# Hybrid encoder step: attention products of 64 rows made with 128 rows

## The chip, the cores and the metric

The kernel runs on one core of one Trainium2 chip. A core has a matrix engine, TensorE (PE in the profile, its weight loads PEld), two engines that work on rows of 128 partitions, VectorE (DVE) and ScalarE (ACT), a programmable engine, GpSimd (POOL), and SyncE (SP), which issues DMAs. Each engine takes its instructions in order; semaphores hold an instruction until another engine's is done. TensorE multiplies a stationary operand of up to 128 rows and 128 columns (the weights, loaded by an instruction of their own) with a moving one; the rows are the partitions over which the product is summed. The metric is the device time of the program in microseconds (us), lower is better.

## The reference

One step of a two-layer streaming encoder: 512 tokens of a new stream (the prompt) and 64 tokens of a running one (the sample, with 256 cached keys). Layer 0 joins a matrix memory and retention, layer 1 is latent attention with 8 heads, and a SwiGLU network and a layer norm follow each. The change is in layer 1's attention:

```python
def block(args):
    qn, qr, qp = args
    s = jnp.einsum('bqhd,bkhd->bhqk', qn, k_nope) + jnp.einsum('bqhr,bkr->bhqk', qr, kr_all)
    s = s.astype(jnp.float32) * MLA_SCALE
    vis = k_chunk[None, :] <= (qp // CHUNK)[:, None]
    p = jax.nn.softmax(jnp.where(vis, s, -jnp.inf), axis=-1).astype(v.dtype)
    return jnp.einsum('bhqk,bkhv->bqhv', p, v)
```

A head's query and key have a part of 128 (`qn`, `k_nope`) and a rotary part of 64 (`qr`, `kr_all`, the key's part being the same for all heads). `CHUNK` is 64: a block of 128 queries sees all keys up to its end, except that its first 64 queries don't see the last 64 keys.

## The kernel before

All products are made in pieces: an operand is split into a high part (fp32r) and a low part (what is left of it), and a product is the sum of high x high, high x low and low x high. The 576 tokens stand in five tiles: tile 0 is the sample with 64 tokens, tiles 1 to 4 are the prompt with 128 each. Weights come from memory by DMA, ScalarE and VectorE (or GpSimd, in the stretch of the attention, `lo_engine`) split them into the two parts (line 364 and 362), and a ring of slots holds them.

In the attention each head has three kinds of work. `heads(h)` makes its keys and queries (`kn_units`, `qn_units`) and brings the rotary queries into place (`qr_unit`): `qrt[h % 2]` has 128 partitions, in one half the high part of the 64 rotary values, in the other half their low part; for odd heads the halves are swapped (`p0 = 64 * (h % 2)`). The rotary keys stand twice, in partitions 0 to 63 and again in 64 to 127: `kk` has the high part, `self.kl[0]` the low part. `values(p)` makes the values of two heads: `vt[0]` and `vt[1]` have the two parts for seven tiles of keys (`KTILE`); the third of them holds the sample's last keys, 64 rows of them.

`attn(h)` spawns one task per tile, and each has three steps:
- `sa(i)`: the scores. Five products go into one bank: three of 128 rows for the large part, one of 128 rows with `kk` (queries' high and low part with the keys' high part), and one of 64 rows, the queries' high part with the keys' low part (line 1958). For the prompt's tiles a sixth product of one row (line 1960) adds -1e30 to the last 64 keys of the first 64 queries: `mrow` is a row of bf16 numbers, made at the kernel's start. Then VectorE takes the maximum (line 1963), ScalarE the exponential (1964), and GpSimd or VectorE divides by the sum (1967).
- `sb(i)`: TensorE transposes the probabilities (line 533), ScalarE and VectorE split them into two parts (1879, 1880). For the sample these are `pt0`, with three blocks of keys; of the third only 64 rows are written.
- `sc(i)`: probabilities times values. For the sample there are nine products, of which the three with the last keys have `w` = 64 rows.

The order of all this is written once, when the program is made: the tasks yield to a planner that adds up an assumed time of each product (`clk` in `mm`) and resumes a task when its lag is over. The recorded order then stands in each engine's queue.

Of the kernel before, what the change touches and what calls it, by code (L numbers as in the profile page):

```python
# [8 lines left out]
F32 = mybir.dt.float32  # L9
F32R = mybir.dt.float32r  # L10
BF16 = mybir.dt.bfloat16
# [17 lines left out]
NEG = -1.0e30  # L29
# [188 lines left out]
class Kern:  # L218
# [335 lines left out]
    def setup(self):  # L554
        nc, t = self.nc, self.t
        self.lead = LEAD
        self.lo_engine = nc.vector
        self.tk = TK0
        self.Z = self.st("Z", [128, KT * NTOK])
        self.T0 = self.st("T0", [128, T0_N])  # L560
        self.T1 = self.st("T1", [128, T1_N])
        self.Xh = self.st("Xh", [128, KT * NTOK], F32R)
        self.Xl = self.st("Xl", [128, KT * NTOK], F32R)
        self.H = self.st("H", [128, 2 * KT * NTOK], F32R)
        self.small = self.st("small", [128, 480])
        self.sm_at = 0
        self.ident = self.st("ident", [128, 128])
        self.ones = self.st("ones", [128, 128])
        self.cvec = self.st("cvec", [128, 4])
        self.lnv = self.st("lnv", [128, 4, 2, 8])  # L570
        self.gv = self.st("gv", [128, 8])
        self.mask = self.st("mask", [128, 2, 128])
        self.rope = self.st("rope", [128, 2, NT, 64])
        self.cst = self.st("cst", [128, 12])
        self.bif = self.st("bif", [128, 8])
        self.mrow = self.st("mrow", [1, 192], BF16)
        nc.gpsimd.memset(self.ones, 1.0 / 1024.0)
        nc.gpsimd.memset(self.cvec[:, 0:2], 1.0 / 1024.0)
        nc.gpsimd.memset(self.cvec[:, 2:4], 1.0 / 512.0)
        nc.gpsimd.memset(self.mrow[:, 0:64], 1.0)  # L580
        nc.gpsimd.memset(self.mrow[:, 64:128], 0.0)
        nc.gpsimd.memset(self.mrow[:, 128:192], NEG)
        wg = self.T0[:, 4300:4364]
        self.wgp = self.st("wgp", [128, KT, 16], F32R)
        for j in range(4):
            for k in (2 * j, 2 * j + 1) if j == 0 else (2 * j,):
                e = k + 1 if j == 0 else k + 2
                nc.sync.dma_start(half_view(self.Z, 0, k, e), half_dram(t["x"], 0, k, e))
                if j < RAW and k % 2 == 0:
                    self.dma_w(j, 2 if j == 0 else 1)  # L590
        nc.gpsimd.dma_start(wg, t["wg"])
        for name in ("rope", "mask", "cst", "ident"):
            nc.gpsimd.dma_start(getattr(self, name), t[name])
        nc.gpsimd.dma_start(self.bif, t["b_if"].to_broadcast([128, 8]))
# [1068 lines left out]
    def layer1(self):  # L1663
        nc, t = self.nc, self.t
        V, A, G = nc.vector, nc.scalar, nc.gpsimd
        T0, H = self.T0, self.H
# [195 lines left out]
        pt0 = knt[1][:, :, 832:1024].rearrange("p b (j q) -> p b j q", j=3)  # L1862
        qnt = [T1r[:, 832 + 1152 * j:832 + 1152 * (j + 1)].rearrange("p (a t) -> p a t", a=2) for j in range(2)]
        qrt = [T1r[:, 3136 + 576 * j:3712 + 576 * j] for j in range(2)]
        KTILE = [(0, 128), (128, 128), (256, 64)] + [(320 + 128 * j, 128) for j in range(4)]

        late = []
# [70 lines left out]
        def attn(h):  # L1938
            qn, kn = qnt[h % 2], knt[h % 2]
            qs = qrt[h % 2]  # L1940
            p0 = 64 * (h % 2)
            vc = 128 * (h % 2)
            obank = {}

# [3 lines left out]
            def sa(i):  # L1948
                L, s = TLEN[i], TSTART[i]
                k0, k1, _ = keys(i)  # L1950
                n = k1 - k0
                x = self.xbank()
                ps = x[0:L, 0:n]
                self.mm(ps, qn[:, 0, s:s + L], kn[:, 0, k0:k1], True, False)
                self.mm(ps, qn[:, 0, s:s + L], kn[:, 1, k0:k1], False, False)
                self.mm(ps, qn[:, 1, s:s + L], kn[:, 0, k0:k1], False, False)
                self.mm(ps, qs[:, s:s + L], kk[:, k0:k1], False, False)
                self.mm(ps, qs[p0:p0 + 64, s:s + L], self.kl[0][p0:p0 + 64, k0:k1], False, i == 0)
                if i:
                    self.mm(x[:, n - 64:n], self.mrow[:, 0:128], self.mrow[:, 128:192], False, True)  # L1960
                nm, den = self.smalls(1)[0:L], self.smalls(1)[0:L]
                P = Pb[(5 * h + i) % 3][0:L, 0:n]
                V.tensor_reduce(nm, ps, AX.X, ALU.max, negate=True)
                A.activation(P, ps, AF.Exp, bias=nm, accum_out=den)
                flush()
                V.reciprocal(den, den)
                (G if i in NP else V).tensor_scalar(P, P, den, None, ALU.mult)
# [25 lines left out]
            def sc(i):  # L1993
# [15 lines left out]
                for gi, (c, n, q0, ts, j0) in enumerate(groups):  # L2009
                    seq, late = [], []  # L2010
                    for j, tt in enumerate(ts):
                        w = KTILE[tt][1]
                        vh, vl = vt[0][0:w, tt, vc:vc + 128], vt[1][0:w, tt, vc:vc + 128]
                        a, b = full[0][0:w, j0 + j, q0:q0 + n], full[1][0:w, j0 + j, q0:q0 + n]
                        seq += [(vh, a), (vl, a)]
                        late.append((vh, b))
                    seq += late
# [227 lines left out]
```

## Time and profile before

| | before |
|---|---|
| median of 3 runs | 1423.02 us (1422.81 to 1429.33) |
| the profiled execution | 1427.26 us |
| its span, first to last instruction | 1425.3 us |
| TensorE busy | 1387.2 us (97%) |
| VectorE, ScalarE, GpSimd busy | 971.2, 611.9, 171.1 us |
| attention of layer 1 | 800 to 956 us of the span |

The profile is of one execution. The ends of TensorE's products are modelled, and they overlap: the sum of their lengths says little, and what a product costs is read from the start of the one behind it. Most of TensorE's products are issued from one line (465, in the helper `mm`) and all transposes from line 533, so that they are told apart by the names of their operands and by their shape.

### The profile page before, as it was taken

The numbers are of one execution on the slowest core, as the hardware profiler recorded it, in microseconds if no ns is written. First come the engines' busy times: TensorE is split into PE (matmuls) and PEld (weight loads), VectorE is DVE, ScalarE is ACT, GpSimd is POOL, SyncE is SP. The second block draws the span as 40 slices with busy tenths as digits, with TensorE's granted clock in tenths as the row PEclk, the third lists the DMA queues.
The fourth block names the chain that finished last, engine by engine and source line by source line (L and its number), as shares of the span: only waits on it lengthen the run. The fifth ranks groups of instructions, "written<-read, shape, count | busy, mean of one in ns | idle before, by whom it ended". The sixth has DMA issues, their size and how long they took to land.

```text
span 1425.3 us, 24687 instructions
## 1 busy us (share of the span) xinstructions
PE 1387.2 (97%) x9787; PEld 1312.4 (92%) x9787; DVE 971.2 (68%) x2252; ACT 611.9 (43%) x1295; POOL 171.1 (12%) x203
## 2 busy tenths in 40 slices
PE   7999999999999999999999999999999999999995
PEld 5767999998999999999987888889899999999995
DVE  5645577767973576488898555557888458747876
ACT  4411333435551353255354455543555235415543
POOL 5200010104200000000021433310230000000000
PEclk9998999999999999999999999999999999999998
DMA  6111121522233122322321100012212313322221
GB/s 213 60 60 37 60 60 60 176 70 60 75 104 104 60 89 91 102 89 91 116 84 57 33 28 31 31 47 73 89 45 89 135 45 105 104 77 87 90 74 67
DMA packets 37314, 112.91 MB, mean 79 GB/s; under 512 B 4504, under 2 KB 11608, under 8 KB 37200
## 3 DMA queue, kind: packets, MB, share of 16 engines
q1 hardware_dynamic: 36656, 110.33, 23.2%
q8 instruction: 76, 1.25, 0.3%
q0 software_dynamic: 544, 1.02, 0.2%
q14 instruction: 38, 0.31, 0.1%
HBM read 107.45 MB, written 3.89 MB: 78 GB/s over the span
## 4 chain that ended last, share of the span: by engine, by line
PE 86%; DVE 8%; ACT 2%; DMA 1%; issue 1%; POOL 1%; SPq 0%; POOLq 0%; ACTq 0%; DVEq 0%
PE mm L465 45%; PE x L465 38%; PE x L533 2%; DVE r L362 1%; DVE Z L1270 1%; PE o L465 1%; DVE Z L1256 1%; DMA raw<-in_w 1%; ACT Xh L1302 1%; DMA Z<-in_x 0%; ACT Z L1309 0%; ACT r L364 0%; DVE small L543 0%; DVE small L542 0%; DVE small L541 0%
## 5 line engine op out<-in xcount | busy, mean ns | idle before, releaser
L465 PE MATMUL mm<-H,r 128*128 128x320 f32 (+2 forms) x2832 | 388.6, 296 | 0.0
L465 PEld LDWEIGHTS mm<-H,r 128*128 128x128 f32 x2832 | 379.1, 188 | 0.7
L465 PE MATMUL x<-Xh,r 128*128 128x288 f32 x1216 | 243.6, 295 | 0.0
L465 PE MATMUL mm<-Xh,r 128*128 128x288 f32 (+2 forms) x1152 | 232.1, 299 | 6.1 <-DVE Z L1176 2.7
L364 ACT CAST r<-raw 128x512 fp32r<-128x512 f32 (+2 forms) x292 | 178.0, 646 | 110.1 <-PE mm L465 78.9
L362 DVE TENSOR_TENSOR r<-raw,r 128x512 fp32r<-128x512 f32 (+2 forms) x276 | 195.8, 738 | 41.7 <-ACT r L364 38.0
L465 PE MATMUL x<-r,r 128*128 128x288 f32 (+3 forms) x1534 | 212.0, 293 | 0.2 <-DVE r L1046 0.2
L465 PEld LDWEIGHTS x<-r,r 128*128 128x128 f32 (+1 forms) x1534 | 205.1, 188 | 1.7 <-issue 0.7
L465 PEld LDWEIGHTS x<-Xh,r 128*128 128x128 f32 x1216 | 194.5, 188 | 0.5
L465 PEld LDWEIGHTS mm<-Xh,r 128*128 128x128 f32 x1152 | 185.4, 191 | 7.5 <-ACT Z L1309 3.4
L465 PE MATMUL x<-Xl,r 128*128 128x288 f32 x608 | 179.0, 294 | 0.0
L465 PE MATMUL mm<-Xl,r 128*128 128x288 f32 (+2 forms) x576 | 168.6, 301 | 0.0
L364 ACT CAST r<-T 128x512 fp32r<-128x512 f32 (+1 forms) x114 | 86.8, 761 | 126.9 <-DVE T L397 103.6
L465 PEld LDWEIGHTS x<-Xl,r 128*128 128x128 f32 x608 | 114.1, 188 | 0.0
L465 PEld LDWEIGHTS mm<-Xl,r 128*128 128x128 f32 x576 | 108.4, 191 | 0.1
L362 DVE TENSOR_TENSOR r<-T,r 128x512 fp32r<-128x512 f32 (+1 forms) x114 | 96.3, 866 | 17.8 <-ACT r L364 17.8
L465 PE MATMUL mm<-r,Xh 128*128 128x512 f32 (+1 forms) x320 | 100.5, 396 | 6.9 <-ACT r L364 5.8
L1310 POOL TENSOR_TENSOR Xl<-Z,Xh 128x288 fp32r<-128x288 f32 (+2 forms) x36 | 30.7, 853 | 468.0 <-ACT Z L1309 467.8
L465 PEld LDWEIGHTS mm<-r,Xh 128*128 128x128 f32 x320 | 59.8, 195 | 20.5 <-ACT r L364 6.6
L1214 ACT ACTIVATE T<-Z 128x288 f32<-128x288 f32 (+2 forms) x56 | 24.8, 443 | 92.1 <-DVE Z L1176 47.3
L465 PE MATMUL mm<-r,Xl 128*128 128x512 f32 (+1 forms) x160 | 62.2, 389 | 0.0
L1571 DVE TENSOR_TENSOR T<-T,x 128x288 f32<-128x288 f32 x38 | 17.3, 454 | 59.8 <-PE x L465 59.8
(315 smaller groups left out, 1738.8 us busy)
## 6 DMA issues: line engine op xcount, KB each, us to landing
raw<-in_w SPq DMA_DIRECT2D x169, 512.0 KB, 3.6
r<-in_w SPq DMA_DIRECT2D x20, 512.0 KB, 3.6
Z<-in_x SPq DMA_DIRECT2D x1, 1280.0 KB
o_y<-Z SPq DMA_DIRECT2D x2, 640.0 KB, 3.2
Z<-in_x SPq DMA_DIRECT2D x2, 512.0 KB, 5.9
Z<-in_x SPq DMA_DIRECT2D x1, 1024.0 KB, 8.8
o_y<-Z SPq DMA_DIRECT2D x4, 256.0 KB, 2.2
Z<-in_x SPq DMA_DIRECT2D x3, 320.0 KB, 9.3
```

Of the source, the lines that this page charges most:

```text
L362: self.lo_engine.tensor_tensor(t[:, 1], src, t[:, 0].bitcast(F32), ALU.subtract)
L364: self.nc.scalar.copy(t[:, 0], src)
L465: self.nc.tensor.matmul(out, lhsT, rhs, start=start, stop=stop, skip_group_check=more)
L533: self.nc.tensor.transpose(out, in_, self.ident[0:n, 0:n])
L1214: nc.scalar.activation(q, z, AF.Square)
L1256: V.tensor_tensor(z, z, xd[:, 0:n], ALU.subtract)
L1270: V.scalar_tensor_tensor(z, z, gain(m), R[:, 0:n], ALU.mult, ALU.mult)
L1302: A.activation(self.Xh[:, a:b], z, AF.Identity, bias=bias(m))
L1310: G.tensor_tensor(self.Xl[:, a:b], z, self.Xh[:, a:b].bitcast(F32), ALU.subtract)
L1571: V.tensor_tensor(s[:, 0:n], s[:, 0:n], ps, ALU.add)
```

## The change

The products of 64 rows and of one row in the attention are made with 128 rows.
- The low rotary product takes all 128 partitions of `qs` and of `self.kl[0]`. With it the queries' low part times the keys' low part is added, which was left out before.
- The mask is a piece of `H` with 128 partitions and 192 columns of fp32r, zero but for the first partition. The row `mrow` in bf16 and its three fills at the start are gone.
- The products of the sample's last keys take 128 rows of `vt` and of `pt0`. GpSimd fills the rows 64 to 127 of both with zeros ahead of the first head; nothing else is written there afterwards.

```diff
--- before.py
+++ after.py
@@ -573,13 +573,9 @@
         self.rope = self.st("rope", [128, 2, NT, 64])
         self.cst = self.st("cst", [128, 12])
         self.bif = self.st("bif", [128, 8])
-        self.mrow = self.st("mrow", [1, 192], BF16)
         nc.gpsimd.memset(self.ones, 1.0 / 1024.0)
         nc.gpsimd.memset(self.cvec[:, 0:2], 1.0 / 1024.0)
         nc.gpsimd.memset(self.cvec[:, 2:4], 1.0 / 512.0)
-        nc.gpsimd.memset(self.mrow[:, 0:64], 1.0)
-        nc.gpsimd.memset(self.mrow[:, 64:128], 0.0)
-        nc.gpsimd.memset(self.mrow[:, 128:192], NEG)
         wg = self.T0[:, 4300:4364]
         self.wgp = self.st("wgp", [128, KT, 16], F32R)
         for j in range(4):
@@ -1862,6 +1858,14 @@
         pt0 = knt[1][:, :, 832:1024].rearrange("p b (j q) -> p b j q", j=3)
         qnt = [T1r[:, 832 + 1152 * j:832 + 1152 * (j + 1)].rearrange("p (a t) -> p a t", a=2) for j in range(2)]
         qrt = [T1r[:, 3136 + 576 * j:3712 + 576 * j] for j in range(2)]
+
+
+        for a in [pt0[64:128, p, 2] for p in range(2)] + [t[64:128, 2] for t in vt]:
+            G.memset(a.bitcast(F32), 0.0)
+        mask = H[:, 8768:8960]
+        G.memset(mask.bitcast(F32), 0.0)
+        G.memset(mask[0:1, 0:64].bitcast(F32), 1.0)
+        G.memset(mask[0:1, 128:192].bitcast(F32), NEG)
         KTILE = [(0, 128), (128, 128), (256, 64)] + [(320 + 128 * j, 128) for j in range(4)]
 
         late = []
@@ -1938,7 +1942,6 @@
         def attn(h):
             qn, kn = qnt[h % 2], knt[h % 2]
             qs = qrt[h % 2]
-            p0 = 64 * (h % 2)
             vc = 128 * (h % 2)
             obank = {}
 
@@ -1955,9 +1958,9 @@
                 self.mm(ps, qn[:, 0, s:s + L], kn[:, 1, k0:k1], False, False)
                 self.mm(ps, qn[:, 1, s:s + L], kn[:, 0, k0:k1], False, False)
                 self.mm(ps, qs[:, s:s + L], kk[:, k0:k1], False, False)
-                self.mm(ps, qs[p0:p0 + 64, s:s + L], self.kl[0][p0:p0 + 64, k0:k1], False, i == 0)
+                self.mm(ps, qs[:, s:s + L], self.kl[0][:, k0:k1], False, i == 0)
                 if i:
-                    self.mm(x[:, n - 64:n], self.mrow[:, 0:128], self.mrow[:, 128:192], False, True)
+                    self.mm(x[:, n - 64:n], mask[:, 0:128], mask[:, 128:192], False, True)
                 nm, den = self.smalls(1)[0:L], self.smalls(1)[0:L]
                 P = Pb[(5 * h + i) % 3][0:L, 0:n]
                 V.tensor_reduce(nm, ps, AX.X, ALU.max, negate=True)
@@ -2009,9 +2012,8 @@
                 for gi, (c, n, q0, ts, j0) in enumerate(groups):
                     seq, late = [], []
                     for j, tt in enumerate(ts):
-                        w = KTILE[tt][1]
-                        vh, vl = vt[0][0:w, tt, vc:vc + 128], vt[1][0:w, tt, vc:vc + 128]
-                        a, b = full[0][0:w, j0 + j, q0:q0 + n], full[1][0:w, j0 + j, q0:q0 + n]
+                        vh, vl = vt[0][:, tt, vc:vc + 128], vt[1][:, tt, vc:vc + 128]
+                        a, b = full[0][:, j0 + j, q0:q0 + n], full[1][:, j0 + j, q0:q0 + n]
                         seq += [(vh, a), (vl, a)]
                         late.append((vh, b))
                     seq += late
```

No instruction changes its place in a queue. TensorE's queue in the first head, the end of tile 1's scores and those of tile 2, with the semaphores that are waited for (the width is that of the output, the number of rows isn't shown; `x` is the scores' bank, `T_434` and `T_433` the queries and low keys), before:

```order
L465 MATMUL x_8085<-H_74,T_434_7587 128x128
L465 MATMUL x_8085<-T_434_7587 128x128
L465 LDWEIGHTS mrow_85
L465 MATMUL x_8085<-mrow_85 128x64
L465 MATMUL x_8096<-r_454_7909,T_434_7587 128x256 [waits PE_49]
L465 MATMUL x_8096<-r_454_7909,T_434_7587 128x256 x2
L465 MATMUL x_8096<-H_74,T_434_7587 128x256
L465 MATMUL x_8096<-T_434_7587 128x256
L465 LDWEIGHTS mrow_85
```

and in the changed kernel:

```order
L465 MATMUL x_8088<-H_74,T_433_7583 128x128
L465 MATMUL x_8088<-T_433_7583 128x128
L465 MATMUL x_8088<-H_74 128x64 [waits Pool_49]
L465 MATMUL x_8099<-r_453_7905,T_433_7583 128x256 [waits PE_49]
L465 MATMUL x_8099<-r_453_7905,T_433_7583 128x256 x2
L465 MATMUL x_8099<-H_74,T_433_7583 128x256
L465 MATMUL x_8099<-T_433_7583 128x256
```

The mask is one instruction with a load like that of its neighbours, from `H`, where a bf16 load and a product stood, and its first product waits for GpSimd.

GpSimd's queue between the rotated queries (the last `T` ahead) and the low parts of the first head's weights (`r` from `raw`), before:

```order
L1851 TENSOR_TENSOR T_2_70<-T_2_70 128x512 [waits DMAHW3_49,DMAHW5_49,DVE_49,PE_49]
L1851 TENSOR_TENSOR T_2_70<-T_2_70 128x512 [waits DMAHW6_49,DMAHW4_49,DVE_49]
L1851 TENSOR_TENSOR T_2_70<-T_2_70 128x512 [waits DMAHW6_49,DMAHW7_49,DVE_49,PE_49]
L362 TENSOR_TENSOR r_27_126<-raw_442_7707,r_27_126 128x512 [waits DMAHW1_49,Activation_49]
L362 TENSOR_TENSOR r_31_175<-raw_443_7719,r_31_175 128x512 [waits DMAHW2_49,PE_49,Activation_49]
```

and in the changed kernel:

```order
L1847 TENSOR_TENSOR T_2_70<-T_2_70 128x512 [waits DMAHW6_49,DMAHW4_49,DVE_49]
L1847 TENSOR_TENSOR T_2_70<-T_2_70 128x512 [waits DMAHW6_49,DMAHW7_49,DVE_49,PE_49]
L1864 MEMSET r_454_7906 64x64 [waits Pool_49]
L1864 MEMSET r_454_7906 64x64
L1864 MEMSET r_455_7907 64x256
L1864 MEMSET r_456_7908 64x256 [waits DMASW1_49]
L1866 MEMSET H_74 128x192 [waits Pool_49]
L1867 MEMSET H_74 1x64 [waits Pool_49]
L1868 MEMSET H_74 1x64
L362 TENSOR_TENSOR r_26_122<-raw_441_7703,r_26_122 128x512 [waits DMAHW1_49,Activation_49]
L362 TENSOR_TENSOR r_30_171<-raw_442_7715,r_30_171 128x512 [waits DMAHW2_49,PE_49,Activation_49]
```

The seven fills stand ahead of three splits of weights, and none of them waits for another compute engine. The queues of VectorE, ScalarE and SyncE are the same.

## Rows read from the trace of the kernel before

**Rows 1.** The page of the profile: busy time of each engine with its share of the span, and the shares of the engines in the chain of work that ended last.

```profile
PE 1387.2 (97%) x9787; PEld 1312.4 (92%) x9787; DVE 971.2 (68%) x2252; ACT 611.9 (43%) x1295; POOL 171.1 (12%) x203
...
PE 86%; DVE 8%; ACT 2%; DMA 1%; issue 1%; POOL 1%; SPq 0%; POOLq 0%; ACTq 0%; DVEq 0%
```

**Rows 2.** The table of stretches, the one from 800 to 956 us (the attention): length, then busy time of PE, PEld, DVE, ACT and POOL with the number of instructions that started in it, then the granted TensorE clock, the DMA share and GB/s.

```profile
800.00:956.00 156.00, 156.00 (x1057) 133.89 (x1056) 83.29 (x227) 81.18 (x233) 47.28 (x45) 1.00 0.09 28
```

**Rows 3.** The timeline of TensorE (PE) in the first head, in order of time; columns: start in us, us from the first start to the last end of the row's instructions, engine, line, operation, output <- inputs, rows*columns of the weights, shape of the moving operand, count. `T` holds the scaled queries and the keys' low part (buffer T1), `r` the keys' two parts (buffer `knt`), `H` the rotary keys' high part, `x` the scores. A row of several instructions has only the first start. 802.74 to 803.41 is the sample's group, 803.70 to 804.55 that of tile 1, 804.67 to 805.66 that of tile 2; 805.79 belongs to the key projection of the next head. 810.44 lies in the group of tile 3, 811.20 begins that of tile 4, and 812.89 comes behind it.

```profile
802.74 0.60 PE L465 MATMUL x<-r,T 128*64 128x320 f32 x3
803.18 0.30 PE L465 MATMUL x<-H,T 128*64 128x320 f32 x1
803.41 0.35 PE L465 MATMUL x<-T 64*64 64x320 f32 x1
803.70 0.55 PE L465 MATMUL x<-r,T 128*128 128x128 f32 x3
804.09 0.28 PE L465 MATMUL x<-H,T 128*128 128x128 f32 x1
804.29 0.32 PE L465 MATMUL x<-T 64*128 64x128 f32 x1
804.55 0.20 PE L465 MATMUL x<-mrow 1*128 1x64 bf16 x1
804.67 0.63 PE L465 MATMUL x<-r,T 128*128 128x256 f32 x3
805.14 0.28 PE L465 MATMUL x<-H,T 128*128 128x256 f32 x1
805.35 0.38 PE L465 MATMUL x<-T 64*128 64x256 f32 x1
805.66 0.20 PE L465 MATMUL x<-mrow 1*128 1x64 bf16 x1
805.79 3.70 PE L465 MATMUL mm<-H,r 128*128 128x256 f32 x26
...
810.44 0.34 PE L465 MATMUL x<-H,T 128*128 128x384 f32 x1
...
811.20 0.97 PE L465 MATMUL x<-r,T 128*128 128x512 f32 x3
...
812.89 0.74 PE L465 MATMUL mm<-H,r 128*128 128x256 f32 x4
```

**Rows 4.** The timeline of TensorE in narrow stretches, so that a row begins with an instruction in the midst of its run: the same columns.

```profile
803.86 0.39 PE L465 MATMUL x<-r,T 128*128 128x128 f32 x2
...
806.13 0.52 PE L465 MATMUL mm<-H,r 128*128 128x256 f32 x3
...
806.49 0.58 PE L465 MATMUL mm<-H,r 128*128 128x256 f32 x3
...
810.09 0.51 PE L465 MATMUL x<-r,T 128*128 128x384 f32 x2
...
811.77 0.40 PE L465 MATMUL x<-r,T 128*128 128x512 f32 x1
812.01 0.40 PE L465 MATMUL x<-H,T 128*128 128x512 f32 x1
...
814.50 0.39 PE L465 MATMUL o<-r,r 128*128 128x64 f32 x2
```

**Rows 5.** The timeline of TensorE's weight loads (PEld) in the groups of tile 1: the same columns.

```profile
804.03 0.19 PEld L465 LDWEIGHTS x<-H,T 128*128 128x128 f32 x1
804.29 0.18 PEld L465 LDWEIGHTS x<-T 64*128 64x128 f32 x1
804.54 0.09 PEld L465 LDWEIGHTS <-mrow 1*128 1x128 bf16 x1
804.67 0.42 PEld L465 LDWEIGHTS x<-r,T 128*128 128x128 f32 x3
```

**Rows 6.** The timeline of TensorE at the nine products of probabilities and values for the sample, of the first head (814.39) with the product behind them (first of two at 815.83, third at 816.23), and of the sixth head (910.93) with the transposes behind them: the same columns.

```profile
814.39 1.51 PE L465 MATMUL o<-r,r 128*128 128x64 f32 x9
...
815.83 0.56 PE L465 MATMUL mm<-H,r 128*128 128x320 f32 x2
...
816.23 0.46 PE L465 MATMUL mm<-H,r 128*128 128x320 f32 x2
...
910.93 1.42 PE L465 MATMUL o<-r,r 128*128 128x64 f32 x9
912.29 0.44 PE L533 MATMUL x<-ident,T 128*128 128x128 f32 x2
```

**Rows 7.** The timeline of GpSimd (POOL) between the rotated queries and the first low parts of weights (the last bracket: idle time before, and what ended it), and the view of line 975, a fill: count, then shortest, median and longest duration in ns, first and last start.

```profile
791.28 1.29 POOL L1851 TENSOR_TENSOR T<-T 128x512 f32<-128x512 f32 x1 [1.09 <-PE mm L465]
792.52 1.29 POOL L362 TENSOR_TENSOR r<-raw,r 128x512 fp32r<-128x512 f32 x1
796.01 1.30 POOL L362 TENSOR_TENSOR r<-raw,r 128x512 fp32r<-128x512 f32 x1 [2.19 <-ACT r L364]
...
L975 POOL MEMSET Z<- x1: 307/307/307, 53.0 to 53.0; 64x256 f32 x1
```

**Rows 8.** The timeline of VectorE (DVE) and of TensorE at the second head's first score product: the scaled rotary queries that VectorE writes, and the product.

```profile
815.71 0.83 DVE L1920 SCALAR_TENSOR_TENSOR T<-x,T 64x320 fp32r<-64x320 f32 x2
...
817.77 0.39 PE L465 MATMUL x<-r,T 128*64 128x320 f32 x1
```

## The prediction

> **What bounds the kernel now.** I read the page's busy times and its chain of work first, then the table of stretches, then the attention instruction by instruction. TensorE is busy for 97% of the span and holds 86% of the chain that ended last [rows 1]. The change touches only the attention, 800 to 956 us. There TensorE is busy for all 156.0 us, VectorE for 83.3, ScalarE for 81.2 and GpSimd for 47.3, and the granted clock is 1.00, the upper level of 2.4 GHz [rows 2]. So TensorE's own instructions set the end here: a product that takes a shorter time on TensorE shortens the kernel, as long as nobody else becomes late.
>
> A busy TensorE doesn't mean that every product is cheap. The lengths in the rows overlap, so a product's price is read from the distance between two starts. In an undisturbed run of products of 128 rows it is 0.115 us at 128 columns and 0.12 at 256 (803.86 to 804.09 for two, 806.13 to 806.49 for three), 0.11 at 64, 0.175 at 384, 0.24 at 512 [rows 3, 4], and 0.147 at 320 (802.74 to 803.18 for three) [rows 3]. Now the scores of the first head's tile 1: three products, the one with the keys' high part, the rotary low product of 64 rows, the mask product of 1 row. From 804.09 to 804.29 passes 0.20 us instead of 0.11, from 804.29 to 804.55 0.26 instead of 0.11, the mask takes 0.12, and the first product of the next group, 256 wide, is late as well: 805.79 to 806.13 for two products, behind tile 2's mask, is 0.34 instead of 0.24 [rows 3, 4]. The weight loads show why: in an even run a load starts ahead of its product (804.03 for the product of 804.09), but the loads of the 64-row product, of the mask and of the next 128-row product start at 804.29, 804.54 and 804.67, with their products and not ahead of them [rows 3, 5]. Wherever the number of rows changes, the load of the next weights isn't covered by the product before it.
>
> **The change part by part.** Three kinds of products get 128 rows: the low rotary product (one in each of 5 tiles and 8 heads, 40), the mask (32), and the three products of each head with the sample's last 64 keys (24). The program's order stays; only the 32 separate weight loads of the mask go, and seven fills on GpSimd come.
>
> Scores. I compare what the first head's groups take with what the same products take at the plain distances.
> - Sample, 803.18 to 803.70: two products of 320 columns in 0.52, plain 0.29. Saves 0.23.
> - Tile 1, 803.70 to 804.67: six products in 0.97, plain 6 x 0.11 = 0.66. Saves 0.31.
> - Tile 2, 804.67 to 805.79: 1.12, plain 5 x 0.12 + 0.11 = 0.71. Saves 0.41. The product behind its mask: 0.10.
> - Tile 3: its first three products stand behind transposes that stay, so I count only 810.44 to 811.20, 0.76, plain 2 x 0.175 + 0.11 = 0.46. Saves 0.30.
> - Tile 4, 811.20 to 812.89: 1.69, plain 5 x 0.24 + 0.11 = 1.31. Saves 0.38, and 0.10 for the product behind it, by the same reading as tile 2.
>
> Together 1.83 us [rows 3, 4]. In these plain times the mask with 128 rows of fp32r weights is priced at the 0.11 of another 64-column product of that kind, from 814.39 to 814.50 [rows 4, 6]; its bounds are 0.11 and the 0.12 that it takes now.
>
> Values. The nine products of the sample take 1.44 us (814.39 to 815.83); three of them have 64 rows, in two places, so the number of rows changes four times. Plain is 9 x 0.11 = 0.99, so 0.45 is saved, and the product behind them, 320 wide, is late by 0.10 (815.83 to 816.23 for two is 0.40, plain 0.29). In heads 1, 3 and 5 transposes follow instead; head 5's nine products take 1.36 (910.93 to 912.29), which saves 0.37, and I count nothing behind them [rows 6].
>
> Sum: 5 heads x (1.83 + 0.55) + 3 heads x (1.83 + 0.37) = 11.9 + 6.6 = 18.5 us. The transposes of the sample's 64 rows keep their changes of height, and none is counted.
>
> GpSimd. The seven fills stand between the last addition for the rotated queries (791.28) and the low part of a weight block (792.52) in its queue. Four have 64 partitions and 64 or 256 columns, one has 128 x 192, two have one partition. A fill of 64 x 256 took 0.31 us [rows 7], so seven take at most 7 x 0.31 = 2.2. Behind them wait the low-part splits from 792.52 on. The first split ended at 793.81, and TensorE's first product that waits for it comes after 806.49 [rows 4, 7]: 12.7 us of cover, so I take zero. The second split has had 2.2 us of idle time ahead of it, which swallows the fills. Without that cover 2.2 us would be lost once. The mask's first reader, at 804.55, now waits for the fills too, which end by about 795. At the kernel's start three small fills are gone from GpSimd's queue; TensorE doesn't wait for GpSimd there, so nothing is counted.
>
> What is late next. TensorE now arrives earlier at products that wait for VectorE and ScalarE, whose work isn't shortened. The tightest place that I found among the groups that change is the second head's first score product, 817.77, whose queries VectorE had finished at 816.54 at the latest: 1.23 us [rows 8]. TensorE gains 0.10 + 0.45 + 0.10 between tile 4's scores and this product, so 0.6 us of cover is left there; since the other engines' queues don't move up by all that TensorE gained earlier, I take a new wait of 0.2 us once; bounds 0 and 1.5 (0.2 in each head).
>
> Total: 18.5 - 0.2 = 18.3 us. From the profiled execution's 1427.3 us that makes 1409.0; that execution is 4.2 above the median of the runs, 1423.0, and the edit's worth doesn't hang on that. **Forecast: 1423.0 - 18.3 = 1404.7 us.** Bounds of the cost terms: if the first product behind a score group stays late (4 x 0.10 a head, 3.2 in all) and the waits cost 1.5, the gain is 14.0 and the time 1409.0; if every head gains the first head's 2.38 and nothing waits, it is 19.0, 1404.0.
>
> **The rivals.**
> (a) *The waits take it back.* VectorE and ScalarE are busy for a little over half of this stretch [rows 2], but each softmax is a chain of four steps on three engines between a score group and its transposes. If in each head one such chain ends late by what the groups ahead of it gained (about half of the 2.4), 9 us come back: 1414. Against it: the covers above are longer than the gains in front of them.
> (b) *Height isn't the cause.* The low product reads both operands from one tile, and the mask is bf16 between fp32r products; either could be what breaks the run. Then the widened low product keeps its price and only the values, with neither, gain 8 x 0.45 = 3.6: 1419. Against it: the values' 64-row products, fp32r from the same tiles as their 128-row neighbours, break the run just as long (0.45 for four changes) [rows 6].
> (c) *Slower: the widened product's load is not covered.* If a 128-row load can't run under the product before it, each of the 96 products pays its load of 0.18 us [rows 5] besides its 0.11 or more. Where the neighbours stay late too, the 32 masks cost 0.29 instead of 0.12 (5.4 us) and the 24 values' products 0.29 instead of about 0.19 (2.4), the low products about the same: 1431. It decides from some 0.19 us a widened product (18.3 / 96), where the gain is gone. Against it: the rows in which 128-row loads start ahead, at distances of 0.11 to 0.12 [rows 3 to 5].
> The Trainium skill ("TensorE: Matmul & The Clock Gate", Part 3, "The mechanism" and "What overlaps and what doesn't") speaks against this change: a weight load overlaps a running product only where their row groups differ, and 128 rows share all of them; it also names a background weight buffer that lets a load go ahead. By the first half alone rival (c) and its 1431 would hold; the load of 804.03 disagrees with that half.
>
> **How the numbers follow.** Forecast 0.85; (a) 0.07; (b) 0.05; (c) 0.03. A measurement of this kernel can tell about 0.5%, 7.1 us. The forecast and nearly all of (a), at -0.6%, are faster by more than that; (b) lies within. Faster 0.91, same 0.06, slower 0.03. The range takes the bounds 1404.0 to 1409.0 and some us for the scatter of the runs, which reached from 0.2 below to 6.3 above their median: 1401 to 1410. It leaves out (a), (b), (c), 0.15 in all.
>
> **What would show it.** In the profile after, the distances behind the high-part product, the low product and the mask should be 0.11 to 0.24 by width, tile 1's group 0.66 and tile 2's 0.71; the sample's nine products about 1.0; the loads of the low product and of the mask should start ahead of their products. The stretch from the first score to the last value should be 18 us shorter, TensorE still busy for all of it, with no wait for VectorE, ScalarE or GpSimd above 0.3 us. Wrong would be a mask at 0.29 (c), a low product still at 0.26 to 0.43 (b), or idle time of TensorE ahead of the transposes or the first score product of a head (a).

## The result and the profile after

| | before | after |
|---|---|---|
| median of 6 runs each | 1423.05 us | 1404.84 us |
| ratio | | 0.9873, 95% interval 0.9854 to 0.9892 |
| span of the profiled execution | 1425.3 us | 1402.7 us |
| transposes of the attention, first to last start | 155.3 us | 136.4 us |

The kernel is faster by 18.2 us (1.3%; the interval reaches from 15.4 to 20.8 us); forecast were 18.3. In a second set of six executions of the kernel after, one was slow at 2667.46 us, for a reason that the record doesn't show, and the figures below leave it out. The last row of the table is the measure that the rest of this text goes by. It is one row of a view: all products that TensorE made from the identity and the tile `T` (the rotated queries and the probabilities), with their count, their shortest, median and longest duration in ns and their first and last start. The first of them stands ahead of the first head's scores and the last behind the last head's, so the distance between the two, 955.7 - 800.4 and 931.5 - 795.1, is the length of the attention; the runs' scatter of several us doesn't enter it. Its ends are rounded to 0.1 us, so a difference of two such lengths can be off by 0.2. Before:

```profile
L533 PE MATMUL x<-ident,T x144: 216/272/331, 800.4 to 955.7; 128*128 128x128 f32 x112, 64*128 64x64 f32 x24, 64*64 64x64 f32 x8
```

After:

```profile
L533 PE MATMUL x<-ident,T x144: 216/272/332, 795.1 to 931.5; 128*128 128x128 f32 x112, 64*128 64x64 f32 x24, 64*64 64x64 f32 x8
```

The attention is 18.9 us shorter. The two profiled executions differ by 22.6 in their spans, and the rest, 3.7, isn't the change's: ahead of the attention the execution of before is 5.3 later (800.4 against 795.1), behind it 1.6 shorter. Most of the 5.3 is the clock: in the stretch from 110 to 126 us, where nothing was changed, TensorE was granted 0.68 in the profiled execution of before and 1.00 in that of after. The table of stretches, the columns as in [rows 2], before:

```profile
110.00:126.00 16.00, 14.33 (x50) 9.63 (x49) 7.60 (x34) 1.61 (x3) 0.00 (x0) 0.68 0.00 0
```

and after:

```profile
110.00:126.00 16.00, 14.31 (x72) 9.71 (x71) 7.65 (x34) 1.61 (x3) 0.34 (x2) 1.00 0.00 1
```

TensorE was busy for 14.3 of these 16 us in both, but with 50 products that started in one and 72 in the other, so the execution of before came out of this stretch late. 1.00 is the upper level of 2.4 GHz throughout; 0.68 is a mean over time at it and at 1.2 GHz. So a few us of a profile's span must not be read as an edit's worth.

The page after says the same as the first row of [rows 1], with 22 us less of busy TensorE:

```profile
PE 1364.9 (97%) x9787; PEld 1307.0 (93%) x9787; DVE 969.1 (69%) x2252; ACT 612.1 (44%) x1295; POOL 172.1 (12%) x207
```

The first head's scores on TensorE's timeline after, to be read beside [rows 3] (columns as there; 797.83 to 798.12 is the end of the sample's group, 798.12 begins tile 1, 798.70 tile 2, 804.00 to 804.35 the end of tile 3, 804.38 tile 4, 807.12 the sample's values):

```profile
797.83 0.31 PE L465 MATMUL x<-H,T 128*64 128x320 f32 x1
798.12 0.45 PE L465 MATMUL x<-r,T 128*128 128x128 f32 x3
798.40 0.28 PE L465 MATMUL x<-H,T 128*128 128x128 f32 x1
798.51 0.27 PE L465 MATMUL x<-T 128*128 128x128 f32 x1
798.62 0.24 PE L465 MATMUL x<-H 128*128 128x64 f32 x1
798.70 0.60 PE L465 MATMUL x<-r,T 128*128 128x256 f32 x3
...
804.00 0.34 PE L465 MATMUL x<-H,T 128*128 128x384 f32 x1
804.17 0.34 PE L465 MATMUL x<-T 128*128 128x384 f32 x1
804.35 0.19 PE L465 MATMUL x<-H 128*128 128x64 f32 x1
804.38 0.93 PE L465 MATMUL x<-r,T 128*128 128x512 f32 x3
...
805.65 0.72 PE L465 MATMUL mm<-H,r 128*128 128x256 f32 x4
...
807.12 1.17 PE L465 MATMUL o<-r,r 128*128 128x64 f32 x9
808.13 0.54 PE L465 MATMUL mm<-H,r 128*128 128x320 f32 x2
```

All weights in these rows now have 128 rows. Tile 1's group takes 0.58 (798.12 to 798.70), where it took 0.97, and tiles 3 and 4 are shorter in the same way. The low product comes 0.11 us after the high-part product in tile 1 (798.40 to 798.51) and 0.17 in tile 3 (804.00 to 804.17), by its width, and is followed after the same. The mask shows something that the plain distances had not: behind it the next start comes after 0.03 us (804.35 to 804.38; 0.08 in tile 1, 798.62 to 798.70), not after 0.11. Part of what is missing is taken by the products behind: tile 4's first three take 0.77 (804.38 to 805.15), 0.05 more than their plain 0.72. Over its whole group, which begins behind one mask and ends with another, tile 4 takes 1.27 (804.38 to 805.65), and plain were 1.31: a mask costs a little less than the 0.11 that was priced. The nine products of the values take 1.01 us (807.12 to 808.13) instead of 1.44 [rows 6].

The weight loads of tile 1 (PEld), the rows that answer to [rows 5]:

```profile
798.34 0.19 PEld L465 LDWEIGHTS x<-H,T 128*128 128x128 f32 x1
798.45 0.19 PEld L465 LDWEIGHTS x<-T 128*128 128x128 f32 x1
798.56 0.19 PEld L465 LDWEIGHTS x<-H 128*128 128x128 f32 x1
798.67 0.42 PEld L465 LDWEIGHTS x<-r,T 128*128 128x128 f32 x3
```

The loads of the low product (798.45), the mask (798.56) and the next group (798.67) start 0.06, 0.06 and 0.03 ahead of their products, where they had started with them. Among wider products the lead is longer: in tile 2's group the low product's load starts at 799.14 and its product at 799.26.

GpSimd's fills, to be read beside [rows 7]:

```profile
787.31 0.73 POOL L1864 MEMSET r<- 64x64 f32 x4
788.10 0.27 POOL L1866 MEMSET H<- 128x192 f32 x1
788.42 0.14 POOL L1867 MEMSET H<- 1x64 f32 x1
788.51 0.14 POOL L1868 MEMSET H<- 1x64 f32 x1
788.62 1.28 POOL L362 TENSOR_TENSOR r<-raw,r 128x512 fp32r<-128x512 f32 x1
790.71 1.29 POOL L362 TENSOR_TENSOR r<-raw,r 128x512 fp32r<-128x512 f32 x1 [0.80 <-ACT r L364]
```

They take from 787.31 to 788.62, 1.31 us, and the split behind them starts at once. The next split still has 0.80 us of idle time ahead of it, where it had 2.19: the fills were taken out of that. In the attention TensorE waited for GpSimd nowhere. From 795 to 945 us the view of waits (who waited for whom, us in total, times, longest) has one line for TensorE, a wait for VectorE behind the attention's last transposes, and of before it has the same 0.8 us there, on line 1176:

```profile
PE mm L465 <- DVE Z L1172: 0.8, 1, 0.8
```

### The profile page after: what moved, and what is told of

Its sections match the earlier page's. It is cut to its first block, busy times and chain, and to the rows that moved or that the text cites. A ratio compares the mean times of both kernels' runs of the same rounds, so it can differ in the third digit from the quotient of the medians.

```text
span 1402.7 us, 24691 instructions
## 1 busy us (share of the span) xinstructions
PE 1364.9 (97%) x9787; PEld 1307.0 (93%) x9787; DVE 969.1 (69%) x2252; ACT 612.1 (44%) x1295; POOL 172.1 (12%) x207
## 4 chain that ended last, share of the span: by engine, by line
PE 85%; DVE 9%; ACT 2%; DMA 1%; issue 1%; POOL 1%; SPq 0%; POOLq 0%; ACTq 0%; DVEq 0%
PE mm L465 45%; PE x L465 37%; PE x L533 2%; DVE r L362 2%; DVE Z L1266 1%; DVE Z L1252 1%; DMA raw<-in_w 1%; PE o L465 1%; ACT Xh L1298 1%; ACT Z L1305 0%; DMA Z<-in_x 0%; ACT r L364 0%; DVE small L541 0%; DVE small L543 0%; DVE small L542 0%
```

## The experiments

Ten kernels more, all measured by the stretch of the transposes, since most of the differences are smaller than the scatter of the runs. Under each stands its row of the same view as above, and the diffs show only the lines that change. Nearly all rest on one profiled execution each. The kernel after, run once more, gave 136.5 us (934.8 - 798.3), a median of 1404.83 over five executions and 0.9849 of before (0.9823 to 0.9875).

> The changed kernel itself, for comparison on the same chip: 0.987 of the kernel before, the transposes' stretch 136.4 us.

### One part alone

The low product alone with 128 rows:

```diff
-                self.mm(ps, qs[p0:p0 + 64, s:s + L], self.kl[0][p0:p0 + 64, k0:k1], False, i == 0)
+                self.mm(ps, qs[:, s:s + L], self.kl[0][:, k0:k1], False, i == 0)
```

> Only the low rotary product has 128 rows; mask (1 row) and values (64 rows) as before. Measure in all runs: from the first to the last start of the attention's transposes, 155.3 us before and 136.4 us with all three parts. If each change of height between neighbouring products costs time, the sample's visit to 64 rows goes (8 x 0.29 = 2.3) and of a prompt group's three changes one goes: 32 x (0.41 - 0.21) = 6.4, so 146.6 (145.5 to 148). If the 64-row product is dear by itself and the mask costs nothing, the 40 products give back 40 x 0.29 + 32 x 0.1 and it is about 140.

The row of the transposes in this run:

```profile
L533 PE MATMUL x<-ident,T x144: 216/273/331, 797.8 to 944.3; 128*128 128x128 f32 x112, 64*128 64x64 f32 x24, 64*64 64x64 f32 x8
```

146.5 us (944.3 - 797.8): 8.8 saved, forecast 8.7. From here to the kernel after 10.1 are left; less the 3.8 of the values below that is 6.3 for the mask of one row in 32 groups, about 0.2 us each, as was read from the rows.

The mask alone:

```diff
+        mask = H[:, 8768:8960]
+        G.memset(mask.bitcast(F32), 0.0)
+        G.memset(mask[0:1, 0:64].bitcast(F32), 1.0)
+        G.memset(mask[0:1, 128:192].bitcast(F32), NEG)
-                    self.mm(x[:, n - 64:n], self.mrow[:, 0:128], self.mrow[:, 128:192], False, True)
+                    self.mm(x[:, n - 64:n], mask[:, 0:128], mask[:, 128:192], False, True)
```

> Only the mask has 128 rows; the low product keeps 64, the values too. A prompt group still goes 128 to 64 to 128, with its mask now on the way back: the mask's product saves one of three changes, 32 x 0.10 to 0.13 = 3.2 to 4.2, so the transposes' stretch is 151.1 to 152.1 us instead of 155.3. If a mask of one row in another number format was the whole cost behind the low product, 32 x (0.10 to 0.20 ahead of it + 0.02 + 0.10 behind it) go, 147 or less.

The row of the transposes in this run:

```profile
L533 PE MATMUL x<-ident,T x144: 216/272/329, 801.5 to 956.0; 128*128 128x128 f32 x112, 64*128 64x64 f32 x24, 64*64 64x64 f32 x8
```

154.5 us (956.0 - 801.5): 0.8 saved instead of 3.2 to 4.2. This expectation failed, for both of the theories in it. Beside the low product of 64 rows the mask's height is worth almost nothing, 0.02 us a group.

The values alone:

```diff
+        for a in [pt0[64:128, p, 2] for p in range(2)] + [t[64:128, 2] for t in vt]:
+            G.memset(a.bitcast(F32), 0.0)
-                        w = KTILE[tt][1]
-                        vh, vl = vt[0][0:w, tt, vc:vc + 128], vt[1][0:w, tt, vc:vc + 128]
-                        a, b = full[0][0:w, j0 + j, q0:q0 + n], full[1][0:w, j0 + j, q0:q0 + n]
+                        vh, vl = vt[0][:, tt, vc:vc + 128], vt[1][:, tt, vc:vc + 128]
+                        a, b = full[0][:, j0 + j, q0:q0 + n], full[1][:, j0 + j, q0:q0 + n]
```

> Only the values' products of the sample's last keys have 128 rows. These are fp32r on both sides and read the same tiles as their neighbours, so neither a change of format nor a shared tile can be at work. By the height: 5 x 0.55 + 3 x 0.37 = 3.9, so the stretch is 151.4 us (151.0 to 151.8) instead of 155.3. If height isn't the cause, 155.3.

The row of the transposes in this run:

```profile
L533 PE MATMUL x<-ident,T x144: 216/273/329, 797.4 to 948.9; 128*128 128x128 f32 x112, 64*128 64x64 f32 x24, 64*64 64x64 f32 x8
```

151.5 us (948.9 - 797.4): 3.8 saved, forecast 3.9.

The parts alone save 8.8, 0.8 and 3.8, together 13.4; all three save 18.9. The 5.5 that are missing belong to the mask: with the low product already at 128 rows it is worth 18.9 - 8.8 - 3.8 = 6.3, with the low product at 64 it is worth 0.8. What counts is whether a group stays at 128 rows from its beginning to its end.

### The order alone

The value products of the sample in another order, the three of 64 rows side by side; no product changes:

```diff
+                    seq.sort(key=lambda p: p[0].shape[0] == 64)
```

> The kernel before with the order of the nine value products of the sample changed: the six of 128 rows first, then the three of 64 rows side by side, so two changes of height go and the products stay the same. If the change costs, and not the product of 64 rows, 0.21 to 0.23 a head are saved, 1.7 to 1.8 in all: 153.5 us instead of 155.3. If a product of 64 rows is dear by itself, 155.3.

The row of the transposes in this run:

```profile
L533 PE MATMUL x<-ident,T x144: 216/272/331, 798.4 to 951.7; 128*128 128x128 f32 x112, 64*128 64x64 f32 x24, 64*64 64x64 f32 x8
```

153.3 us (951.7 - 798.4), 2.0 saved, forecast 1.7 to 1.8, which is the same within the rounding.

The low product moved away from the mask, so that each group leaves 128 rows twice:

```diff
+                self.mm(ps, qs[p0:p0 + 64, s:s + L], self.kl[0][p0:p0 + 64, k0:k1], False, False)
-                self.mm(ps, qs[:, s:s + L], kk[:, k0:k1], False, False)
-                self.mm(ps, qs[p0:p0 + 64, s:s + L], self.kl[0][p0:p0 + 64, k0:k1], False, i == 0)
+                self.mm(ps, qs[:, s:s + L], kk[:, k0:k1], False, i == 0)
```

> The kernel before with the low product moved ahead of the high-part rotary product, so that a prompt group goes 128, 64, 128, 1, 128: four changes of height and not three, with the same products. If the change costs: 32 x about 0.19 and 8 x about 0.08 for the sample, where a wide product follows now: 162 us instead of 155.3 (160 to 163). If the products cost by themselves, 155.3.

The row of the transposes in this run:

```profile
L533 PE MATMUL x<-ident,T x144: 215/273/330, 797.9 to 958.6; 128*128 128x128 f32 x112, 64*128 64x64 f32 x24, 64*64 64x64 f32 x8
```

160.7 us (958.6 - 797.9), 5.4 longer; forecast were 6.7 (4.7 to 7.7). The same products, in the first of these two runs with two changes of height fewer a head and in the second with one visit more a group: the cost lies in the changes and not in the small products. Nor does it matter in which half of the partitions the 64 rows stand: in the kernel before, the product behind tile 1's low product starts 0.26 us after it in all eight heads, though the odd heads use the other half.

### The mask's format, height and place

The kernel after with its mask in bf16, 128 rows:

```diff
+        self.mrow = self.st("mrow", [128, 192], BF16)
+        nc.gpsimd.memset(self.mrow, 0.0)
+        nc.gpsimd.memset(self.mrow[0:1, 0:64], 1.0)
+        nc.gpsimd.memset(self.mrow[0:1, 128:192], NEG)
-        mask = H[:, 8768:8960]
-        G.memset(mask.bitcast(F32), 0.0)
-        G.memset(mask[0:1, 0:64].bitcast(F32), 1.0)
-        G.memset(mask[0:1, 128:192].bitcast(F32), NEG)
-                    self.mm(x[:, n - 64:n], mask[:, 0:128], mask[:, 128:192], False, True)
+                    self.mm(x[:, n - 64:n], self.mrow[:, 0:128], self.mrow[:, 128:192], False, True)
```

> The changed kernel, with its mask in bf16 (128 rows, zero but for the first). If the height is the cause, the format between fp32r neighbours doesn't matter: the stretch of the transposes stays at 136.4 us (135.5 to 136.6; the bf16 load is 0.09 us instead of 0.18). If the change of format breaks the run, the mask's visit costs about 0.2 again in 32 groups: 143.

The row of the transposes in this run:

```profile
L533 PE MATMUL x<-ident,T x144: 216/273/328, 796.1 to 932.6; 128*128 128x128 f32 x112, 64*128 64x64 f32 x24, 64*64 64x64 f32 x8
```

136.5 us (932.6 - 796.1), as after: at 128 rows the format between fp32r neighbours costs nothing.

The kernel before with the mask as an fp32r product of the low product's 64 rows:

```diff
+        mask = H[:, 8768:8960]
+        G.memset(mask.bitcast(F32), 0.0)
+        for r in (0, 64):
+            G.memset(mask[r:r + 1, 0:64].bitcast(F32), 1.0)
+            G.memset(mask[r:r + 1, 128:192].bitcast(F32), NEG)
-                    self.mm(x[:, n - 64:n], self.mrow[:, 0:128], self.mrow[:, 128:192], False, True)
+                    self.mm(x[:, n - 64:n], mask[p0:p0 + 64, 0:128], mask[p0:p0 + 64, 128:192], False, True)
```

> The kernel before with the mask as an fp32r product of the same 64 rows as the low product, so a prompt group changes height twice (128, 64, 64, 128) and not three times. If every change has the same price, 32 x 0.13 = 4.2 go: 151 us instead of 155.3. If the price is the weight load that isn't covered, what goes is only the mask's short bf16 load (0.09), and the next product's fp32r load was uncovered before as well: 32 x 0.02 to 0.08 = 0.6 to 2.6, so 152.7 to 154.7.

The row of the transposes in this run:

```profile
L533 PE MATMUL x<-ident,T x144: 216/273/331, 797.5 to 949.7; 128*128 128x128 f32 x112, 64*128 64x64 f32 x24, 64*64 64x64 f32 x8
```

152.2 us (949.7 - 797.5): 3.1 saved, 0.10 a group. It lies between the two expectations, nearer to that of the uncovered load (2.6 at most) than to an equal price for each change (4.2), and neither is met.

The run with the mask alone at 128 rows, with the mask ahead of the low product:

```diff
-                self.mm(ps, qs[p0:p0 + 64, s:s + L], self.kl[0][p0:p0 + 64, k0:k1], False, i == 0)
-                    self.mm(x[:, n - 64:n], mask[:, 0:128], mask[:, 128:192], False, True)
+                    self.mm(x[:, n - 64:n], mask[:, 0:128], mask[:, 128:192], False, False)
+                self.mm(ps, qs[p0:p0 + 64, s:s + L], self.kl[0][p0:p0 + 64, k0:k1], False, True)
```

> As the run with only the mask widened, with the mask (128 rows) ahead of the low product (64 rows) instead of behind it: 128, 128, 64, 128. That run saved only 0.8 us, 0.02 a group, though a group had one change of height fewer. Theory V: a visit to 64 rows by one wide product costs about 0.40 a group, whatever stands on its way back; the mask's hop was nearly free. Then this run is at 154.5 us as well (154.0 to 155.3). Theory P: the visit costs 0.31, and the mask spoiled it by standing right behind the change, too short to cover the next load. Then 32 x 0.10 are saved: 152.1 us (151.7 to 152.6).

The row of the transposes in this run:

```profile
L533 PE MATMUL x<-ident,T x144: 216/272/328, 802.0 to 954.4; 128*128 128x128 f32 x112, 64*128 64x64 f32 x24, 64*64 64x64 f32 x8
```

152.4 us (954.4 - 802.0): theory P was right in its number, 0.09 a group against 0.02 in the other place. The programs' times don't show gains of this size: this kernel's one execution took 1427.61 us and that with the mask at 64 rows 1423.70, beside 1422.75 and 1423.09 of the kernel before, and single executions of the kernel before differ by more. The timelines of tile 3 of the first head show where it lies (columns as in [rows 3], each from the high-part product to the first product of tile 4). The mask alone, behind the low product:

```profile
811.40 0.34 PE L465 MATMUL x<-H,T 128*128 128x384 f32 x1
811.66 0.44 PE L465 MATMUL x<-T 64*128 64x384 f32 x1
812.04 0.30 PE L465 MATMUL x<-H 128*128 128x64 f32 x1
812.17 0.94 PE L465 MATMUL x<-r,T 128*128 128x512 f32 x3
```

the same mask ahead of it:

```profile
811.79 0.34 PE L465 MATMUL x<-H,T 128*128 128x384 f32 x1
811.97 0.19 PE L465 MATMUL x<-H 128*128 128x64 f32 x1
812.09 0.44 PE L465 MATMUL x<-T 64*128 64x384 f32 x1
812.46 0.97 PE L465 MATMUL x<-r,T 128*128 128x512 f32 x3
```

the mask with 64 rows:

```profile
807.28 0.34 PE L465 MATMUL x<-H,T 128*128 128x384 f32 x1
807.55 0.44 PE L465 MATMUL x<-T 64*128 64x384 f32 x1
807.83 0.19 PE L465 MATMUL x<-H 64*128 64x64 f32 x1
807.95 0.97 PE L465 MATMUL x<-r,T 128*128 128x512 f32 x3
```

and the low product alone widened:

```profile
807.17 0.34 PE L465 MATMUL x<-H,T 128*128 128x384 f32 x1
807.35 0.34 PE L465 MATMUL x<-T 128*128 128x384 f32 x1
807.62 0.20 PE L465 MATMUL x<-mrow 1*128 1x64 bf16 x1
807.75 0.95 PE L465 MATMUL x<-r,T 128*128 128x512 f32 x3
```

From the first to the last row these are 0.77, 0.67, 0.67 and 0.58 us; before it was 0.76 [rows 3], after 0.38. With the mask ahead, the product before the mask is at its plain distance (0.18), the mask takes 0.12, and nothing more is late until the low product is through: the change to 64 rows is hidden in the time that the mask takes in any case. The change back is not: the low product takes 0.37, 0.20 above its plain distance. With the mask behind, both changes are paid, 0.26 ahead of the low product and 0.38 for the low product, and the mask takes 0.13 besides. That the narrow product's own time is what hides the change is read from these distances and not shown by a run of its own. The weight load alone doesn't tell it: with the mask ahead, too, the low product's load starts with its product, both at 812.09.

### Further: the transposes that still have 64 rows

The sample's rotary queries and probabilities are still transposed with 64 rows, two visits a head. Widened (the added rows hold what other work left there, and the columns that come of them aren't read):

```diff
-                        self.transpose(x[:, o:o + TLEN[i]], qr[0:TLEN[i], i, a * 128:(a + 1) * 128])
+                        self.transpose(x[:, o:o + 128], qr[:, i, a * 128:(a + 1) * 128])
-                    self.transpose(x[0:w, j * L:(j + 1) * L], Pb[(5 * h + i) % 3][0:L, j * 128:j * 128 + w])
+                    self.transpose(x[0:w, j * 128:(j + 1) * 128], Pb[(5 * h + i) % 3][:, j * 128:j * 128 + w])
-                x3 = x[:, 0:n * L].rearrange("p (j q) -> p j q", j=n)
+                x3 = x[:, 0:n * 128].rearrange("p (j q) -> p j q", j=n)[:, :, 0:L]
```

> The changed kernel, with the sample's transposes (rotary queries and probabilities, 64 rows) made with 128 rows as well; the added rows hold what other work left there, and the columns they fill are not read. These are the changes of height that are left: about 8 x 0.14 at the probabilities and 8 x 0.24 at the queries by the distances in the changed kernel, 3.0 in all: the transposes' stretch 133.4 us (133 to 134.5) instead of 136.4, the time 3 us lower than the changed kernel's, too little to be told by the runs alone. If transposes don't pay for a change of height, 136.4.

The row of the transposes in this run:

```profile
L533 PE MATMUL x<-ident,T x144: 270/272/332, 795.7 to 929.9; 128*128 128x128 f32 x136, 128*64 128x128 f32 x8
```

134.2 us (929.9 - 795.7), 2.2 saved, median 1401.46 us, 0.9831 of before (0.9806 to 0.9855). The planner assumes a longer time for a transpose of 128 rows and so wrote another order: tile 2's transposes came ahead of tile 3's scores, too early for the probabilities that GpSimd divides, which the timeline shows:

```profile
804.61 0.44 PE L533 MATMUL x<-ident,T 128*128 128x128 f32 x2 [0.63 <-POOL T L1970]
```

The bracket names the idle time ahead of the transposes and the division on GpSimd that ended it.

The same with the planner told the time that it assumed for 64 rows, so that the order stays that of the kernel after:

```diff
-    def transpose(self, out, in_):
+    def transpose(self, out, in_, rows=None):
-        self.clk += max(n, 64) / 1200.0
+        self.clk += max(rows or n, 64) / 1200.0
-                        self.transpose(x[:, o:o + 128], qr[:, i, a * 128:(a + 1) * 128])
+                        self.transpose(x[:, o:o + 128], qr[:, i, a * 128:(a + 1) * 128], TLEN[i])
-                    self.transpose(x[0:w, j * 128:(j + 1) * 128], Pb[(5 * h + i) % 3][:, j * 128:j * 128 + w])
+                    self.transpose(x[0:w, j * 128:(j + 1) * 128], Pb[(5 * h + i) % 3][:, j * 128:j * 128 + w], L)
```

> The widened transposes in the changed kernel's own order: the planner is told the time that it assumed for 64 rows, so no task moves. In the run before, which let it assume more, the stretch was 134.2 us and TensorE waited 0.63 us for GpSimd ahead of tile 2's transposes, which had come ahead of tile 3's scores. If that wait is what was missing to the expected 133.4, this run is at 133.6 (133.2 to 133.9) with no such wait; if the distances at the transposes were mis-sized, it stays at 134.2. The time is 3 us below the changed kernel's.

The row of the transposes in this run:

```profile
L533 PE MATMUL x<-ident,T x144: 270/272/331, 796.4 to 929.7; 128*128 128x128 f32 x136, 128*64 128x128 f32 x8
```

133.3 us (929.7 - 796.4), 3.1 saved, and the wait is gone. The median is 1400.81 us, 0.9832 of before (0.9811 to 0.9853). This is the best version here by its stretch, 3.1 us under the kernel after; by the runs alone the two are hardly told apart: its interval ends just below that of the kernel after in the table (0.9854 to 0.9892) and overlaps that of its second set (0.9823 to 0.9875).

## Why the prediction was right

- **TensorE as the bound.** It held: 18.9 us fewer in the attention came out as 18.2 in the median. That the median meets the forecast to 0.1 us is luck; the interval is over 5 us wide.
- **The scores.** Read beside the same places after, the sample's last two products take 0.29 (plain 0.29 was forecast), tile 1 0.58 (0.66), tile 2 0.70 (0.71), tile 3's last three 0.38 (0.46), tile 4 1.27 (1.31). The groups end a little sooner than forecast, since the product behind a mask begins early and only part of that is taken back; the mask's 0.11 was a little too much. In tile 1 the first three products are shorter too, 0.28 (798.12 to 798.40) where 0.33 was counted.
- **The values.** 3.8 us by their own run, 3.9 forecast.
- **The sum.** 18.5 forecast, 18.9 measured. The bound below it has a slip: 18.5 less 3.2 and 1.5 is a gain of 13.8 and not of 14.0, which would be 1409.2.
- **GpSimd's fills.** Forecast at no cost under 12.7 us of cover, bounded at 2.2 us; they took 1.31, and TensorE did not wait.
- **What is late next.** This term was wrong, if small. The prediction took 0.2 us for the second head's first score product, and there is no new wait. Its cover did shrink by more than was forecast. The rows that answer to [rows 8], first VectorE's timeline after:

```profile
809.08 0.83 DVE L1924 SCALAR_TENSOR_TENSOR T<-x,T 64x320 fp32r<-64x320 f32 x2
```

and TensorE's:

```profile
810.05 0.68 PE L465 MATMUL x<-r,T 128*64 128x320 f32 x3
```

The product's start moved by 7.7 us (817.77 to 810.05), VectorE's by 6.6 (815.71 to 809.08). By the prediction's own measure, the end of VectorE's row, 0.14 us of the 1.23 are left (809.91 to 810.05) and not 0.6: the 0.6 had counted only what TensorE gained between tile 4's scores and this product, and the 0.2 was set aside because the other engines would not move up by all that was gained earlier. But the end of the row is not what the product waits for. The row holds two instructions, the first for the queries of tiles 0 to 2 (64x320, 0.49 long) and the second for those of tiles 3 and 4, and the sample's products read tile 0. In the last kernel above, with the sample's transposes widened and the order kept, VectorE's row and TensorE's are:

```profile
810.23 0.83 DVE L1924 SCALAR_TENSOR_TENSOR T<-x,T 64x320 fp32r<-64x320 f32 x2
...
810.84 0.68 PE L465 MATMUL x<-r,T 128*64 128x320 f32 x3
```

There the product starts 0.22 us before the row ends (811.06), without a wait. Counted from the end of the first of the two, the cover was 1.57 us before, 0.48 after and 0.12 in that kernel. If the product waits for that first one, which no run shows, a further gain ahead of this place would soon be lost in a wait there.
- **Rival (a)**, the waits: no wait appeared. **Rival (b)**, a cause other than the height: the low product still reads both operands from one tile and is at plain distances, the bf16 mask of 128 rows costs nothing more than the fp32r one, and the values alone gain what the height says. **Rival (c)**, an uncovered load at 128 rows: the loads start ahead of their products.
- **The half sentence of the Trainium skill** ("TensorE: Matmul & The Clock Gate", Part 3, "What overlaps and what doesn't") that a load overlaps a running product only where their row groups differ doesn't hold for these products: loads and products of all 128 rows overlap, at 0.11 us from start to start, and in the rows after each load starts 0.03 us or more ahead of its product. The background weight buffer that the page also names would allow that. The runs don't tell by which way it happens, nor why a load doesn't go ahead where the number of rows changes; that cause stays open.

What I read rightly from the trace was the whole of a group's loss. How it divides among the changes in it I had wrong, as the run with the mask alone showed: the price isn't a sum of one price for each change.

## What to carry to other kernels

In a dense run of products, compare the distances between starts with those of an undisturbed run of the same width: a product over fewer rows than its neighbours cost 0.2 to 0.4 us a visit here, as much as the product itself or more, and with the full 128 rows it costs its plain 0.11 to 0.24. Bring all the products of a group to one height, since of two interruptions that stand side by side, removing the mask's alone gave 0.02 us a group, removing the low product's alone about 0.2, and removing both about 0.4; where the height can't be changed, put the odd products side by side, or a short product ahead of them. Measure such an edit by a stretch of the trace that it bounds, and check the order that a planner writes for it.

## What the runs showed of the hardware

- Where the number of rows changes, a weight load starts with its product; where it doesn't, ahead of it, by 0.03 to 0.06 us in tile 1's group and by 0.12 in tile 2's, whose products are wider.
- The price depends on what stands around the change: raising the mask of one row to 128 saved 6.3 us (a difference of runs) where its neighbours had 128 rows and 0.8 where one of them had 64; the same mask of 128 rows saved 0.02 us behind the 64-row product and 0.09 ahead of it.
- Transposes pay at such a change too: widening the sample's transposes of 64 rows saved 3.1 us in 16 visits, 0.19 each.
- An fp32r product of 64 columns takes 0.11 us in a run, as one of 128 columns does; where it follows a product of 256 columns or more, it is itself followed after 0.03 us, and the products behind take longer, by 0.05 us over tile 4's first three.
